# Dividing the attention by its softmax sums behind the mixing, with the sums turned by TensorE and read back from DRAM

## The chip, the cores and the metric

One core of a Trainium2 chip runs the whole program. The metric is the time of one execution on the device, in microseconds; lower is better. A core has five engines with a queue of instructions each: TensorE (PE in the profile; PEld are its weight loads), VectorE (DVE), ScalarE (ACT), GpSimd (POOL) and SyncE (SP), which issues nearly all transfers between DRAM and the on-chip memory. Matmuls write to PSUM, eight banks of 128 partitions by 512 numbers; the other memory, SBUF, holds everything else.

## The reference

Two residual layers over 512 frames of 1024 channels. Layer 0 mixes frames by a causal pooling, layer 1 by attention over chunks of 64 frames; a gated feed-forward network with a causal convolution follows each. The change lies in the attention of layer 1, 16 heads of 64 channels:

```python
s = jnp.einsum('bqhd,bkhd->bhqk', qc, kb).astype(jnp.float32) * scale + bias[None]
valid = (band_chunk + c - LEFT_CHUNKS) >= 0
s = jnp.where(valid[None, None, None, :], s, -1e30)
p = jax.nn.softmax(s, axis=-1).astype(vb.dtype)
return jnp.einsum('bhqk,bkhd->bqhd', p, vb)
```

The softmax divides each row (a frame that asks, q) by the sum of its exponentials over the frames that are looked at (k). Behind the attention the 16 heads' outputs are joined to 1024 channels and multiplied with the matrix `w_o`.

## The kernel before

Products of full precision are made of three matmuls with numbers split into a high and a low part (`hi` and `lo`; helper `split`, L102 on ACT for the high part and L103 on DVE for the low part; `load_split` loads a weight and splits it, the weights wo of pairs 0 to 5 both parts on POOL, L100 and L103). `mm3` at L123 to L125 issues the three.

The attention runs in the loop of L1430 to L1487, over 64 tiles: 16 heads times 4 row tiles of 128 frames. Two heads are a pair p, 0 to 7. Tile t of a head sees the 128 x (t + 1) frames up to its own. In step i of the loop PE is given, in this order:

- `scores(tile i)`: two matmuls sc (L1394, L1395), then DVE adds the bias B and takes the minimum (L1398), ACT takes Exp with the row's sum (L1400), DVE the reciprocal of the sum (L1401), and ACT multiplies the tile by it (L1402). Numbers of the tile lie as sb, with the frames q on the partitions, so that a sum is one number for each partition.
- `channel_major` in two steps of each pair: queries (zh, z) and keys (kl) of the next pair are turned (zt) and scaled; halves of them are moved over the partitions by four DMAs on SP.
- `turn(tile i - 2)`: transposes of the tile's 128x128 blocks (tp, L1410), so that k lies on the partitions, and a split into pt0h, pt0l or pt1h, pt1l (for the even or odd head).
- `mix(head)`, when tile i - 4 is a head's last: the matmuls oo (L1422) of the values with pt; ACT copies half (ob, L1427) and DVE adds (L1428) into `O2[p]`, a tile o of 128 x 512 with the pair's 128 channels on the partitions and the frames q along the row.

Behind each of these a filler puts other matmuls on PE: the products for queries and keys of the later pairs (qk<-wqk) up to step 35, then the output product (wo<-two,wo_h), 144 matmuls, from about step 35.5 on. The output product of pair p reads the split of `O2[p]`, which lies in two (XS[p] and XS[8 + p]); the split is issued at the end of a step, when the pair's last tile has been mixed (L1481 to L1483).

The order on PE is the one in which the code issues the work (`manual_schedule`). On DVE, ACT, POOL and SP a scheduler sets the order at compile time, by its own estimate of what is ready when. Each engine then works its queue strictly in order.

PSUM: the tags P and Q hold the fillers' products, four banks under the tag S serve sc, zt, tp and oo in turn.

Of the kernel before, what the change touches and what calls it, by code (L numbers as in the profile page):

```python
# [17 lines left out]
F32 = mybir.dt.float32  # L18
F32R = mybir.dt.float32r
AF = mybir.ActivationFunctionType  # L20
# [3 lines left out]
P = 128  # L24
S = 512
# [5 lines left out]
HD = 64  # L31
NPAIR = H // 2
TT = S // P
# [39 lines left out]
def trunk(ctx: ExitStack, tc: tile.TileContext, xt, xT, cols, band, edge, poolw, gv, wout, wqk, wv, wo, rel, out):  # L73
    nc = tc.nc
# [3 lines left out]
    tmp = ctx.enter_context(tc.tile_pool(name="tmp", bufs=1))  # L78
    dram = ctx.enter_context(tc.tile_pool(name="dram", bufs=1, space=bass.MemoryType.DRAM))
# [9 lines left out]
    def psum(tag, name, bufs=2):  # L89
        return ps.tile([P, S], F32, name=name, tag=tag, bufs=bufs)  # L90
# [3 lines left out]
    def g_tile(name):  # L94
        return tmp.tile([P, S], F32, name=name, tag="g", bufs=6)
# [31 lines left out]
    def run(steps):  # L127
        step = None
        for step in steps:
            pass  # L130
        return step
# [9 lines left out]
    def small(name, n, tag="nw"):  # L141
        return tmp.tile([P, n], F32, name=name, tag=f"{tag}{n}", bufs=4)
# [211 lines left out]
    ident = consts.tile([P, P], F32, name="ident")  # L354
    col = consts.tile([P, NCOL], F32, name="col")
    ones = consts.tile([P, 1], F32, name="ones")
    gq = consts.tile([P, 2], F32, name="gq")
    rdram = dram.tile([H, RLEN], F32, name="rdram")
    ET = mybir.EngineType
    with tc.tile_pool(name="start", bufs=1) as sp, tc.manual_schedule(engines={ET.PE, ET.DVE, ET.Activation, ET.Pool, ET.SP}):  # L360
        first, second, acc0 = mixer(sp)

    def ffn(l, first, pool, acc, summed=None, upool=None, hook=None):
# [56 lines left out]
        def early():  # L420
# [6 lines left out]
            for at, (f, k, i) in enumerate(units):  # L427
# [13 lines left out]
                if at == (19, 14)[l]:  # L441

                    order = tc.manual_schedule(engines={ET.DVE, ET.Activation}) if l == 0 else nullcontext()
                    order.__enter__()
# [388 lines left out]
        def tour():  # L833
# [8 lines left out]
            def place(f, k):  # L842

                for word in PLACES[k].split():
                    x, name = word.split(".")
                    step = steps_of(f + "qofn".index(x) - 2).get(name)
                    if step:
                        step()

            for f in range(KIND.index("s"), NF + 2):  # L850
# [10 lines left out]
                for k in range(7):  # L861
                    if (f, k) == (ORDERED, 0):
                        order.enter_context(tc.manual_schedule(engines={ET.DVE, ET.Activation, ET.SP}))
                    place(f, k)
# [50 lines left out]
    def attention(rest, hook, hidden_slots):  # L915
        XS = set2
        O2, V, Z, QK, SM = {}, {}, {}, {}, {}
# [440 lines left out]
        def channel_major(p, i):  # L1358


            zt = psum("S", f"zt{p}_{i}", 4)
            for t in range(TT):
                j = 4 * i + 2 * (p % 2)
                nc.tensor.transpose(zt[:, t * P:(t + 1) * P], Z[p // 2, t][:, j:j + 2, :].rearrange("p h d -> p (h d)"), ident)
            zh, z2 = (big.tile([P, S], F32R, name=f"z{c}{p}_{i}", tag="zqk", bufs=8) for c in "h2")
            zl = None if i else g_tile(f"zl{p}_{i}")
            if i:
                nc.scalar.activation(zh, zt, AF.Copy, scale=gq[:, i:i + 1])
                for e in range(2):
                    hs = slice(e * HD, (e + 1) * HD)  # L1370
                    nc.vector.scalar_tensor_tensor(KL[p % 2][e][hs], zt[hs], gq[hs, i:i + 1], zh[hs].bitcast(F32), op0=OP.mult, op1=OP.subtract)
            else:
                split_scaled(zt, gq[:, i:i + 1], zh, zl)

            nc.gpsimd.tensor_copy(z2[HD:], zh[HD:].bitcast(F32))
            moves = [(z2[:HD], (z2 if i else zl)[HD:]), (zh[HD:], (zh if i else zl)[:HD])]
            for o, x in moves:
                nc.sync.dma_start(o.bitcast(F32), x if x.dtype == F32 else x.bitcast(F32))
            QK[p, i] = (zh, z2)

        def scores(h, t):

            p, e = divmod(h, 2)
            q, k, kl = QK[p, 0][e], QK[p, 1][e], KL[p % 2][e]
            if t == 0:

                base = rdram[h, :]
                for r, n in ((0, S - HD), (HD, S)):
                    nc.sync.dma_start(BT[h % 2][r:r + HD, S - n:], bass.AP(tensor=base.tensor, offset=base.offset + HD, ap=[[1, HD], [1, n]]))
            n = (t + 1) * P  # L1390
            nw = max(n, 256)

            sc = psum("S", f"sc{h}_{t}", 4)
            nc.tensor.matmul(sc[:, :nw], q[:, t * P:n], k[:, :nw], start=True, stop=False)  # L1394
            nc.tensor.matmul(sc[:, :nw], q[:, t * P:n], kl[:, :nw], start=False, stop=True)  # L1395
            SM[h, t] = s_ = heads.tile([P, n], F32, name=f"sb{h}_{t}", tag=f"sb{t}")
            mx = tmp.tile([P, 3], F32, name=f"mx{h}_{t}", tag="mx", bufs=4)
            nc.vector.tensor_tensor_reduce(out=s_[:, :n], in0=sc[:, :n], in1=BT[h % 2][:, :n][:, ::-1], scale=1.0,  # L1398
                                           scalar=3e38, op0=OP.add, op1=OP.min, accum_out=mx[:, 0:1])
            nc.scalar.activation(s_[:, :n], s_[:, :n], AF.Exp, scale=-1.0, bias=mx[:, 0:1], accum_out=mx[:, 1:2])  # L1400
            nc.vector.reciprocal(mx[:, 2:3], mx[:, 1:2])  # L1401
            nc.scalar.activation(s_[:, :n], s_[:, :n], AF.Copy, scale=mx[:, 2:3])  # L1402

        def turn(h, t):

# [7 lines left out]
        def mix(h):  # L1413

            p, e = divmod(h, 2)
            hs = slice(e * HD, (e + 1) * HD)
            oo = psum("S", f"oo{h}", 4)
            if p not in O2:
                O2[p] = heads.tile([P, S], F32, name=f"o2_{p}", tag="o2", bufs=4)
            for c in range(2):  # L1420
                for j in range(TT):
                    nc.tensor.matmul(oo[:, j * P:], V[j, h // 4][:, h % 4].rearrange("p a d -> p (a d)"),  # L1422
                                     PT[e][c][:, 4 * j:3 * j + TT].rearrange("p t q -> p (t q)"),
                                     start=j == 0 and c == 0, stop=j == TT - 1 and c == 1)
            ob = g_tile(f"ob{h}")
            other = slice(HD - e * HD, 2 * HD - e * HD)
            nc.scalar.activation(ob[hs], oo[other], AF.Copy)  # L1427
            nc.vector.tensor_add(O2[p][hs], oo[hs], ob[hs])  # L1428

        r2, late = small("r2", TT), []  # L1430
        closing = ExitStack()
        with tc.tile_pool(name="pre", bufs=1, reuse_waits="tile") as pre:
            with tc.manual_schedule(engines={ET.PE, ET.DVE, ET.Activation, ET.SP}):
                rcol, second = opening(pre)
        heads = closing.enter_context(tc.tile_pool(name="bh", bufs=1, reuse_waits="tile"))
# [9 lines left out]
        with tc.manual_schedule(engines={mybir.EngineType.PE}):  # L1445
            cur, done, kept = 0, 0, 0

            def fill(upto):

                nonlocal cur, done  # L1450
                while cur < len(fillers):
                    g, n, a, b = fillers[cur]
                    due = n * (upto - a) / (b - a)
                    while done < min(due, n):
                        next(g)
                        done += 1
                    if upto < b:
                        return
                    run(g)
                    cur, done = cur + 1, 0  # L1460

            fill(0)
            for i in range(nb + LAG + LAGM):
                steps = []
                if i < nb:
                    steps.append(lambda: scores(*tiles_[i]))
                if i % 8 in CM and i // 8 + 1 < NPAIR:
                    steps.append(lambda: channel_major(i // 8 + 1, CM.index(i % 8)))
                j = i - LAG
                if 0 <= j < nb:  # L1470
                    steps.append(lambda: turn(*tiles_[j]))
                j2 = j - LAGM
                if 0 <= j2 < nb and j2 % TT == TT - 1:
                    steps.append(lambda: mix(tiles_[j2][0]))
                for x, step in enumerate(steps):
                    step()
                    if late and x < 2:
                        late.pop(0)()
                    fill(i + (x + 1) / len(steps))

                while 8 * kept + 7 <= j2 and (cur == 3 or cur == 2 and done >= 24 * (kept // 2 + 1)):  # L1481
                    split(O2[kept], XS[kept], XS[KD + kept])
                    kept += 1  # L1483
            fill(nb + FO)
# [40 lines left out]
    with tc.tile_pool(name="ba", bufs=1, reuse_waits="tile") as big:  # L1525
        rest = attention(rest, hook, hidden_slots)
# [55 lines left out]
```

## Time and profile before

| | |
|---|---|
| median of the runs | 967.28 us (967.24 to 968.49) |
| the profiled execution | 969.2 us, of it the span 967.4 us |
| PE busy | 956.3 us, 99% of the span |
| DVE busy | 849.5 us, 88% |
| ACT busy | 594.0 us, 61% |
| POOL busy | 91.2 us, 9% |
| attention's loop | about 447 to 604 us of the span |

How to read the profile: one execution was recorded, and the span is the time between its first and its last instruction. A row of the timeline holds the start in us, the duration in us, the engine, the line of the code, the operation, the tiles written and read, the shape and, in brackets, how long the engine was idle ahead of it and what it waited for. A row of grouped instructions holds the count, then the busy time in us and the mean duration in ns, then the idle time of the engine ahead of them and what ended it. The names of tiles stand without their numbers: o is the `O2` of any pair. A wait for several semaphores is put down to the one that came last.

### The profile page before, as it was taken

What the parts mean: (1) busy time and instruction counts of PE and PEld (TensorE: products, weight loads), DVE (VectorE), ACT (ScalarE), POOL (GpSimd) and SP (SyncE); (2) the same over time, 40 slices, a digit from 0 to 9 for tenths busy, and PEclk for the clock granted to TensorE, in tenths of its full rate; (3) what the DMA queues carried; (4) which work ended last, traced back from release to release, by engine and by line L of the source; (5) the groups of instructions that cost most, each with busy time, mean ns of one, the idle gap of its engine ahead of it and who ended that gap; (6) DMA issues with size and microseconds to landing.
All of it is one profiled execution on the core that took longest, in us unless ns stands there. A gap on an engine that the chain in (4) does not pass through costs nothing.

```text
span 967.4 us, 13737 instructions
## 1 busy us (share of the span) xinstructions
PE 956.3 (99%) x4958; PEld 810.0 (84%) x4958; DVE 849.5 (88%) x1522; ACT 594.0 (61%) x1023; POOL 91.2 (9%) x81
## 2 busy tenths in 40 slices
PE   8999999999999999999999999999999999999998
PEld 7788988888888888888888777888988888888886
DVE  8999999999899859895786887999999999989953
ACT  7665554655555457466898888656565565456531
POOL 2300000000000000043525441000000000000000
PEclk9999999999999999999999999999999999999999
DMA  9222332332323317024433341332333233332323
GB/s 343 73 97 71 115 108 81 120 120 80 114 79 120 102 48 292 21 66 133 132 113 97 88 117 55 100 109 80 94 115 108 84 120 111 102 104 79 114 79 111
DMA packets 38996, 103.87 MB, mean 107 GB/s; under 512 B 4464, under 2 KB 7936, under 8 KB 38928
## 3 DMA queue, kind: packets, MB, share of 16 engines
q1 hardware_dynamic: 38864, 102.95, 33.0%
q8 instruction: 39, 0.64, 0.3%
q14 instruction: 29, 0.24, 0.1%
q0 software_dynamic: 32, 0.04, 0.0%
q10 hardware_dynamic: 32, 0.00, 0.0%
HBM read 96.65 MB, written 2.14 MB: 102 GB/s over the span
## 4 chain that ended last, share of the span: by engine, by line
PE 87%; DVE 8%; ACT 2%; DMA 1%; issue 1%; SPq 0%; POOL 0%; DVEq 0%; ACTq 0%; POOLq 0%
PE st_m L593 10%; PE out L124 8%; PE out L125 8%; PE out L123 8%; PE st_m L595 5%; PE st_t L593 5%; PE gv L124 4%; PE gv L125 4%; PE gv L123 4%; PE qk L123 3%; PE qk L124 3%; PE qk L125 3%; PE st_t L595 3%; PE st_b L593 3%; PE tp L1410 1%; PE st_b L595 1%
## 5 line engine op out<-in xcount | busy, mean ns | idle before, releaser
L124 PE MATMUL out<-one,ow_h 128*128 128x512 f32 x224 | 88.1, 393 | 0.0
L123 PE MATMUL out<-one,ow_h 128*128 128x512 f32 x224 | 88.0, 393 | 0.0
L125 PE MATMUL out<-one,ow_l 128*128 128x512 f32 x224 | 87.9, 393 | 0.0
L829 DVE TENSOR_TENSOR X<-out,X 128x512 f32<-128x512 f32 (+1 forms) x65 | 44.3, 683 | 45.9 <-PE out L125 45.6
L593 PE MATMUL st_m<-two,g_h 128*128 128x512 f32 x240 | 75.1, 394 | 0.1
L593 PE MATMUL st_m<-h,g_h 128*128 128x512 f32 x240 | 74.1, 390 | 0.0
L392 ACT ACTIVATE ow_h<-wo_r 128x768 fp32r<-128x768 f32 (+1 forms) x56 | 44.4, 794 | 43.4 <-PE out L124 39.8
L407 DVE SCALAR_TENSOR_TENSOR c<-a,col,c 128x511 f32<-128x511 f32 (+1 forms) x76 | 56.8, 749 | 0.0
L593 PEld LDWEIGHTS st_m<-h,g_h 128*128 128x128 f32 x240 | 45.1, 188 | 10.3
L595 PEld LDWEIGHTS st_m<-two,g_l 128*128 128x128 f32 x240 | 45.0, 188 | 9.6
L593 PEld LDWEIGHTS st_m<-two,g_h 128*128 128x128 f32 x240 | 44.0, 188 | 10.4 <-ACT w L602 0.8
L393 DVE TENSOR_TENSOR ow_l<-wo_r,ow_h 128x768 fp32r<-128x768 f32 (+1 forms) x56 | 50.4, 899 | 2.3 <-ACT ow_h L392 2.3
L602 ACT ACTIVATE w<-st_m 128x512 f32<-128x512 f32 x30 | 18.0, 598 | 55.2 <-PE st_m L595 55.2
L595 PE MATMUL st_m<-h,g_l 128*128 128x256 f32 x240 | 48.3, 283 | 0.0
L595 PE MATMUL st_m<-two,g_l 128*128 128x256 f32 x240 | 47.6, 280 | 0.0
L124 PEld LDWEIGHTS out<-one,ow_h 128*128 128x128 f32 x224 | 42.4, 189 | 5.7 <-DVE one L418 0.3
L125 PEld LDWEIGHTS out<-one,ow_l 128*128 128x128 f32 x224 | 42.4, 189 | 5.5
L123 PEld LDWEIGHTS out<-one,ow_h 128*128 128x128 f32 x224 | 42.4, 189 | 5.4
L1398 DVE CUSTOM_DVE_ANT_0 sb<-sc,B 128x128 f32<-128x128 f32 (+1 forms) x64 | 31.1, 486 | 17.9 <-PE sc L1395 13.3
L404 ACT ACTIVATE c<-a,col 128x512 f32<-128x512 f32 x38 | 30.7, 813 | 23.8 <-DVE a L751 22.2
L392 ACT ACTIVATE g_h<-gv_r 128x1024 fp32r<-128x1024 f32 x32 | 33.7, 1055 | 13.5 <-DMA gv_r<-gv 12.9
L1400 ACT ACTIVATE sb<-sb,mx 128x128 f32<-128x128 f32 (+1 forms) x64 | 35.7, 558 | 9.8 <-DVE mx L1398 9.2
(459 smaller groups left out, 3035.7 us busy)
## 6 DMA issues: line engine op xcount, KB each, us to landing
gv_r<-gv SPq DMA_DIRECT2D x86, 512.0 KB, 3.9
wo_r<-wout SPq DMA_DIRECT2D x32, 384.0 KB, 3.1
wo_r<-wout SPq DMA_DIRECT2D x32, 320.0 KB, 2.9
wqk_r<-wqk SPq DMA_DIRECT2D x12, 512.0 KB, 3.5
b<-wv SPq DMA_DIRECT2D x8, 512.0 KB, 6.7
wo_r<-wo SPq DMA_DIRECT2D x8, 512.0 KB, 3.6
xt<-xt SPq DMA_DIRECT2D x4, 512.0 KB, 5.2
X<-xT SPq DMA_DIRECT2D x8, 256.0 KB, 7.5
```

The lines of the kernel that those rows point to most:

```text
L123: yield nc.tensor.matmul(o, sh, mh, start=first, stop=False, **how)
L124: yield nc.tensor.matmul(o, sh, ml, start=False, stop=False, **how)
L125: yield nc.tensor.matmul(o, sl, mh, start=False, stop=last, **how)
L392: nc.scalar.activation(hi[:, :n], raw[:, :n], AF.Copy)
L393: return hi, lo, lambda: nc.vector.tensor_sub(lo[:, :n], raw[:, :n], hi[:, :n].bitcast(F32))
L404: nc.scalar.activation(c, a, AF.Identity, scale=cw[2], bias=cw[3])
L407: nc.vector.scalar_tensor_tensor(c[:, j:], a[:, :S - j], cw[2 - j], c[:, j:], op0=OP.mult, op1=OP.add)
L593: nc.tensor.matmul(o, hi[:, c], B[i, name], start=first and i == 0, stop=False, **how)
L595: nc.tensor.matmul(o[:, 0], lo[:, c], B[i, name][:, 0], start=False, stop=i == 3, **how)
L829: nc.vector.tensor_add(X[d][:, fs], o[:, fs], X[d][:, fs])
L1398: nc.vector.tensor_tensor_reduce(out=s_[:, :n], in0=sc[:, :n], in1=BT[h % 2][:, :n][:, ::-1], scale=1.0, scalar=3e38, op0=OP.add, op1=OP.m ...
L1400: nc.scalar.activation(s_[:, :n], s_[:, :n], AF.Exp, scale=-1.0, bias=mx[:, 0:1], accum_out=mx[:, 1:2])
```

## The change

For pairs 0 to 6 (called 1 to 7 by their count) the tiles are no longer multiplied by the reciprocals of their sums. Exp leaves its row sum in a column of `sums[p]`, 128 x 8, one column for each of the pair's eight tiles, and one reciprocal is taken behind the eighth. The tiles are turned and mixed as they are, and the pair's output o is divided afterwards. There the frames lie along the row, not on the partitions, so the eight columns have to be turned and spread:

- `sums_out(p)`, ahead of the scores of step 8p + 9: PE transposes the 128 x 8 reciprocals to 8 x 128 (rt, a bank of tag S), ACT copies them to rs, SP writes rs to DRAM (rinv, 4 KB).
- `sums_in(p)`, step 8p + 11: two reads of SP bring them back as rb, 128 x 512, each row of 512 repeated over the 64 partitions of its head.
- `scale(p)`, step 8p + 15: POOL multiplies o by rb.

The split of o for pairs 0 to 6 is issued four steps later than before, behind the multiplication. `O2` has three buffers, and had four. Pair 7 keeps its scales and reciprocals. In all PE has 7 transposes more, ACT 56 scales less and 7 copies more, DVE 56 reciprocals less and 7 more, POOL 7 multiplications more, SP 7 writes and 14 reads more.

```diff
-            nc.scalar.activation(s_[:, :n], s_[:, :n], AF.Exp, scale=-1.0, bias=mx[:, 0:1], accum_out=mx[:, 1:2])
-            nc.vector.reciprocal(mx[:, 2:3], mx[:, 1:2])
-            nc.scalar.activation(s_[:, :n], s_[:, :n], AF.Copy, scale=mx[:, 2:3])
+            if p < NPAIR - 1:
+                if e == 0 and t == 0:
+                    sums[p] = tmp.tile([P, 2 * TT], F32, name=f"sums{p}", tag="sums", bufs=2)
+                c = e * TT + t
+                nc.scalar.activation(s_[:, :n], s_[:, :n], AF.Exp, scale=-1.0, bias=mx[:, 0:1], accum_out=sums[p][:, c:c + 1])
+                if c == 2 * TT - 1:
+                    nc.vector.reciprocal(sums[p], sums[p])
+            else:
...
+        def sums_out(p):
+
+            rt = psum("S", f"rt{p}", 4)
+            nc.tensor.transpose(rt[:2 * TT, :P], sums.pop(p), ident)
+            rs = heads.tile([2 * TT, P], F32, name=f"rs{p}", tag="rs")
+            nc.scalar.activation(rs, rt[:2 * TT, :P], AF.Copy)
+            nc.sync.dma_start(rinv[p], rs)
+
+        def sums_in(p):
+
+            RB[p] = heads.tile([P, S], F32, name=f"rb{p}", tag="rb")
+            for b in range(2):
+                nc.sync.dma_start(RB[p][b * HD:(b + 1) * HD], rinv[p, b * TT:(b + 1) * TT, :].rearrange("c q -> (c q)")[None].to_broadcast([HD, S]))
+
+        def scale(p):
+            nc.gpsimd.tensor_mul(O2[p], O2[p], RB.pop(p))
...
-                O2[p] = heads.tile([P, S], F32, name=f"o2_{p}", tag="o2", bufs=4)
+                O2[p] = heads.tile([P, S], F32, name=f"o2_{p}", tag="o2", bufs=3)
...
+                p = (i - 9) // 8
+                if 0 <= p < NPAIR - 1 and (i - 9) % 8 in (0, 2, 6):
+                    (sums_out, sums_in, scale)[(i - 9) % 8 // 2 - (i - 9) % 8 // 6](p)
...
-                while 8 * kept + 7 <= j2 and (cur == 3 or cur == 2 and done >= 24 * (kept // 2 + 1)):
+                while 8 * kept + (11 if kept < NPAIR - 1 else 7) <= j2 and (cur == 3 or cur == 2 and done >= 24 * (kept // 2 + 1)):
```

Where the scheduler puts the split of pair 4's output on DVE. Before, it stood between a turned tile of head 10 (pt0l) and the scores of head 11 (sb_2) (o_4 is pair 4's output, two its low part, sc and sb are tiles of the scores):

```order
L1398 ISA sb_1_5769,mx_1_5770<-sc_1_5766,B_4307 128x256
L1398 ISA mx_1_5770 128x1
L103 TENSOR_TENSOR pt0l<-tp_2_5756,pt0h 128x3x128
L103 TENSOR_TENSOR two_102<-o_4_5605,two_98 128x512
L1401 RECIPROCAL mx_1_5770<-mx_1_5770 128x1
L1398 ISA sb_2_5789,mx_2_5790<-sc_2_5786,B_4307 128x384
```

And now, with the reciprocal over the eight sums of pair 5 (sums) ahead of it:

```order
L1349 TENSOR_TENSOR X_75<-wo_0_5727,X_75 128x512
L103 TENSOR_TENSOR pt1l<-tp_1_5773,pt1h 128x2x128
L1407 RECIPROCAL sums_5593<-sums_5593 128x8
L103 TENSOR_TENSOR two_102<-o_4_5570,two_98 128x512
L1399 ISA sb_0_5809,mx_0_5810<-sc_0_5806,B_4307 128x128
L1399 ISA mx_0_5810 128x1
L1454 TENSOR_TENSOR o_5_5780<-oo_5779,ob_5789 64x512
```

The split moved back, from between two tiles of pair 5 to behind the last tile of that pair, ahead of the scores of head 12 (sb_0).

On POOL, around the multiplication of pair 3's output o_3 (wo_0_h and wo_0_l are the two parts of a weight of the output product, z_0 and z_1 halves of queries and keys). Before:

```order
L1375 CAST z_0_5439<-zh_0_5438 64x512
L100 CAST wo_0_h<-wo_0_r 128x1024
L1375 CAST z_1_5475<-zh_1_5474 64x512
L103 TENSOR_TENSOR wo_0_l<-wo_0_r,wo_0_h 128x1024
L1321 TENSOR_TENSOR z_0_5386<-z_0_5386,qk_y 128x512
```

And now:

```order
L1376 CAST z_0_5411<-zh_0_5410 64x512
L100 CAST wo_0_h<-wo_0_r 128x1024
L1376 CAST z_1_5448<-zh_1_5447 64x512
L1428 TENSOR_TENSOR o_3_5322<-o_3_5322,rb_5427 128x512
L103 TENSOR_TENSOR wo_0_l<-wo_0_r,wo_0_h 128x1024
L1322 TENSOR_TENSOR z_0_5357<-z_0_5357,qk_y 128x512
```

The multiplication came in ahead of wo_0_l, which has to wait for it.

On SP, where a weight of the output product (wo_4_r) is loaded beside the moves of pair 6's queries and keys (z, zh). Before:

```order
L1378 DMA z_0_5684<-zl_0_5685 64x512
L1389 DMA B_4306<-rdram 64x448
L1389 DMA B_4306<-rdram 64x512
L1378 DMA zh_0_5683<-zl_0_5685 64x512
L117 DMA wo_4_r<-wo 128x4x256
L1378 DMA z_1_5714<-z_1_5714 64x512
L1378 DMA zh_1_5713<-zh_1_5713 64x512
```

And now:

```order
L1419 DMA rinv<-rs_5608 8x128
L1425 DMA rb_5665<-rinv 64x512 x2
L1390 DMA B_4307<-rdram 64x448
L1390 DMA B_4307<-rdram 64x512
L1379 DMA z_0_5651<-zl_0_5652 64x512
L1379 DMA zh_0_5650<-zl_0_5652 64x512
L1379 DMA z_1_5682<-z_1_5682 64x512
L1379 DMA zh_1_5681<-zh_1_5681 64x512
L117 DMA wo_4_r<-wo 128x4x256
```

The load of wo_4_r went from between the moves to behind the last of them, and the way of pair 4's reciprocals through DRAM came in ahead of them.

More of the change, by code (lines that the diff above doesn't have):

```diff
@@ L358, in trunk @@
     rdram = dram.tile([H, RLEN], F32, name="rdram")
+    rinv = dram.tile([NPAIR, 2 * TT, P], F32, name="rinv")
     ET = mybir.EngineType
@@ L1399, in scores @@
                                            scalar=3e38, op0=OP.add, op1=OP.min, accum_out=mx[:, 0:1])
-            nc.scalar.activation(s_[:, :n], s_[:, :n], AF.Exp, scale=-1.0, bias=mx[:, 0:1], accum_out=mx[:, 1:2])
-            nc.vector.reciprocal(mx[:, 2:3], mx[:, 1:2])
-            nc.scalar.activation(s_[:, :n], s_[:, :n], AF.Copy, scale=mx[:, 2:3])
+            if p < NPAIR - 1:
[6 more added lines that the diff above has]
+            else:
+                nc.scalar.activation(s_[:, :n], s_[:, :n], AF.Exp, scale=-1.0, bias=mx[:, 0:1], accum_out=mx[:, 1:2])
+                nc.vector.reciprocal(mx[:, 2:3], mx[:, 1:2])
+                nc.scalar.activation(s_[:, :n], s_[:, :n], AF.Copy, scale=mx[:, 2:3])
+        def sums_out(p):
[10 more added lines that the diff above has]
+            nc.gpsimd.tensor_mul(O2[p], O2[p], RB.pop(p))
         def turn(h, t):
@@ L1428, in mix @@
             nc.vector.tensor_add(O2[p][hs], oo[hs], ob[hs])
-        r2, late = small("r2", TT), []
+        r2, late, sums, RB = small("r2", TT), [], {}, {}
         closing = ExitStack()
```

## The prediction

> **What bounds the kernel now.** I read the chain of waits first, then the windows of the attention, then the waits of TensorE (PE), then the timeline at each of them.
>
> ```profile
> PE 87%; DVE 8%; ACT 2%; DMA 1%; issue 1%; SPq 0%; POOL 0%; DVEq 0%; ACTq 0%; POOLq 0%
> ```
>
> PE carries the chain, so an operation taken from ACT or DVE is worth only what PE waited for it. Two windows of the attention's loop show where that is (the columns: us, then busy us and number of PE, PEld, DVE, ACT, POOL, then the granted clock).
>
> ```profile
> 447.00:538.00 91.00, 91.00 (x497) 76.64 (x497) 62.76 (x190) 78.11 (x187) 39.21 (x29) 1.00 0.37 109
> 538.00:604.00 66.00, 61.82 (x347) 50.37 (x346) 55.85 (x159) 55.46 (x141) 24.21 (x19) 1.00 0.31 87
> L1402 ACT ACTIVATE sb<-sb,mx 128x128 f32<-128x128 f32 (+1 forms) x64 | 35.5, 556 | 3.8 <-DVE mx L1401 3.0
> PE tp L1410 <- ACT sb L1402: 3.2, 5, 1.7
> ```
>
> Up to 538 us PE is busy for 91.00 of 91.00 us: what the change takes from ACT there is worth nothing. From 538 to 604 it is idle for 4.18 us. The change removes 56 of the 64 scales (31 us of ACT) and 56 of the 64 reciprocals, but PE waited for a scale only 5 times, for 3.2 us in all (the longest 1.7). These places count, and the sum is made from starts of matmuls.
>
> **The pace of PE.** The price of an added transpose, and of a 512-column matmul without a wait:
>
> ```profile
> 525.59 0.40 PE L125 MATMUL qk<-wqk_h,two 128*128 128x512 f32 x1
> 525.83 0.27 PE L1410 MATMUL tp<-ident,sb 128*128 128x128 f32 x1
> 525.85 0.48 PE L123 MATMUL qk<-wqk_h,two 128*128 128x512 f32 x1
> 526.17 0.39 PE L124 MATMUL qk<-wqk_l,two 128*128 128x512 f32 x1
> 526.40 0.40 PE L125 MATMUL qk<-wqk_h,two 128*128 128x512 f32 x1
> ```
>
> A step from one matmul to the next takes 0.23 to 0.24 (526.17 to 526.40). From 525.59 to 526.40 lie three such steps and one transpose: 0.81 - 3 x 0.23 = 0.12 for the transpose, though its row says 0.27.
>
> **What is removed.** The places in order; behind each pair of rows the distance of the starts less 0.23.
>
> ```profile
> 543.85 0.40 PE L125 MATMUL wo<-two,wo_l 128*128 128x512 f32 x1
> 544.50 0.33 PE L1410 MATMUL tp<-ident,sb 128*128 128x128 f32 x1 [0.25 <-ACT sb L1402]
> ...
> 545.84 0.40 PE L123 MATMUL wo<-two,wo_h 128*128 128x512 f32 x1
> 546.51 0.49 ACT L1402 ACTIVATE sb<-sb,mx 128x256 f32<-128x256 f32 x1
> 547.05 0.44 PE L1410 MATMUL tp<-ident,sb 128*128 128x128 f32 x2 [0.82 <-ACT sb L1402]
> ...
> 564.48 0.40 PE L124 MATMUL wo<-two,wo_h 128*128 128x512 f32 x1
> 565.17 0.35 PE L1394 MATMUL sc<-zh,zh 128*128 128x256 f32 x1 [0.30 <-DMA zh<-zh]
> ...
> 571.84 0.47 PE L124 MATMUL wo<-two,wo_h 128*128 128x512 f32 x1
> 572.34 0.76 PE L1422 MATMUL oo<-pt1h,one 128*128 128x512 f32 x3
> ...
> 578.84 0.40 PE L123 MATMUL wo<-two,wo_h 128*128 128x512 f32 x1
> 580.89 0.43 PE L1410 MATMUL tp<-ident,sb 128*128 128x128 f32 x2 [1.65 <-ACT sb L1402]
> ...
> 586.77 0.40 PE L123 MATMUL wo<-two,wo_h 128*128 128x512 f32 x1
> 587.33 0.33 PE L1410 MATMUL tp<-ident,sb 128*128 128x128 f32 x1 [0.17 <-ACT sb L1402]
> ```
>
> At 544.50 0.42 and at 547.05 0.98: the scale of the tile ended late (the second ran from 546.51, on an ACT that had other work until then), and without a scale the transposes wait for Exp alone, which had ended by then. At 565.17 0.46, a wait for the move of zh. At 572.34 0.27, where DVE and ACT are late with the split in front of the mixing; of it I take 0.2, as both lose work there but keep the split. At 580.89 1.82. At 587.33 0.33: pair 7 keeps its scales, but ACT in front of them has fewer. Sum: 4.2 us.
>
> The wait at 565.17 has its cause on SP:
>
> ```profile
> 557.40 0.54 SPq L117 DMA_DIRECT2D wo_r<-wo  x1
> ...
> 558.70 0.54 SPq L1378 DMA_DIRECT2D zh<-zh  x1
> ```
>
> The move was issued at 558.70, behind a load of 512 KB. In the changed order that load stands behind both moves of that pair, so I take the 0.46 as gone. If the 14 rows new on SP held the move up as long, 0 to 0.46 would stay.
>
> The wait at 580.89 has its cause on DVE and POOL:
>
> ```profile
> 577.28 2.38 POOL L103 TENSOR_TENSOR wo_l<-wo_r,wo_h 128x1024 fp32r<-128x1024 f32 x1
> 577.29 2.92 DVE L103 TENSOR_TENSOR two<-o,two 128x512 fp32r<-128x512 f32 x1
> ...
> L103 DVE TENSOR_TENSOR two<-o,two x8: 682/683/2918, 505.4 to 605.8; 128x512 fp32r<-128x512 f32 x8
> ```
>
> The subtraction two<-o of the split takes 0.683 in the median, and 2.92 here, beside POOL's wo_l: it ends 0.55 behind POOL. What stood behind it on DVE, a reciprocal first, was 2.24 late; PE lost 1.82. So DVE's lateness reaches PE less about 0.42. **This is the term on which the sum turns**, since the change moves two<-o and POOL's operations against each other, and does not part them.
>
> The Trainium skill, "SBUF — State Buffer", section "SBUF: two separate sides", has a rule that speaks against this change: GpSimd and a DVE operation with two inputs from SBUF share a pair of ports, the first holds it for its whole instruction and the other blocks. The rows above agree, 2.92 against 0.683; by that rule each of the seven new multiplications on POOL is one more holder, which is the second rival.
>
> **What is added.** Seven transposes rt on PE, each just ahead of a scores matmul: 7 x 0.12 = 0.84. The sums are complete ahead of each (for pair 5 at about 564.4, below, with rt ahead of 566.74), so they wait for nothing new. Bounds: 0, where PE waits there anyway, and 7 x 0.27 = 1.9 by the row's length.
>
> The Trainium skill, "TensorE: Matmul & The Clock Gate", section "Part 4: PE-mode transpose", gives some 275 ns for one within a kernel; the row's 0.27 agrees, and with it the sum would end 1.1 higher, but the starts show 0.12.
>
> Then the three places where wo_l and DVE meet anew.
>
> ```profile
> 539.97 2.39 POOL L103 TENSOR_TENSOR wo_l<-wo_r,wo_h 128x1024 fp32r<-128x1024 f32 x1
> 541.59 0.70 DVE L1428 TENSOR_TENSOR o<-oo,ob 64x512 f32<-64x512 f32 x1
> 543.92 0.17 DVE L1316 TENSOR_TENSOR qk_a<-qk_s,r 128x32 f32<-128x32 f32 x1
> ...
> L1321 POOL TENSOR_TENSOR z<-z,qk_y 128x512 f32<-128x512 f32 x12 | 12.6, 1082 | 14.6 <-DVE qk_y L1319 14.6
> ```
>
> (a) Pair 3: POOL's multiplication of o_3 stands ahead of wo_l now and waits for the addition that ends at 542.29. It takes 1.08 (like the z rows), so wo_l runs from 543.4 to 545.8 in place of 539.97 to 542.36. DVE's qk_a, two inputs from SBUF, comes at 543.92 and is held 1.8; less 0.42, PE waits 1.4.
>
> ```profile
> 563.39 0.72 ACT L1400 ACTIVATE sb<-sb,mx 128x512 f32<-128x512 f32 x1
> 563.93 2.38 POOL L103 TENSOR_TENSOR wo_l<-wo_r,wo_h 128x1024 fp32r<-128x1024 f32 x1
> 565.69 0.29 DVE L1398 CUSTOM_DVE_ANT_0 sb<-sc,B 128x128 f32<-128x128 f32 x1 [1.26 <-PE sc L1395]
> 566.74 0.28 PE L1394 MATMUL sc<-zh,zh 128*128 128x256 f32 x1
> ```
>
> (b) Pair 4: two<-o_4 moves behind the reciprocal over the sums of pair 5, which waits for the Exp that ends at 564.1. So it starts at about 564.4, inside wo_l (to 566.31), and ends 0.55 behind it, at 566.9. The sb of head 12 behind it began at 565.69: 1.2 late, less 0.42 is 0.8 for PE.
>
> ```profile
> 574.96 0.69 DVE L1428 TENSOR_TENSOR o<-oo,ob 64x512 f32<-64x512 f32 x1
> 576.15 1.04 POOL L100 CAST wo_h<-wo_r 128x1024 fp32r<-128x1024 f32 x1 [2.96 <-issue]
> ```
>
> (c) Pair 5: the multiplication of o_5 waits for the addition that ends at 575.65, and wo_h and wo_l stand behind it: wo_l from 577.8 to 580.2. Two<-o_5, now further back on DVE (at about 578.6), ends at 580.75 in place of 579.3: 1.45, less 0.42 is 1.0. Each of (a) to (c) lies between 0 (DVE arrives outside wo_l) and the 2.24 that the full collision held DVE. I take the values above, from the order and these starts.
>
> The way through DRAM is the new wait for POOL. Nothing in the trace has its shape; the nearest rows:
>
> ```profile
> outT<-X SPq DMA_DIRECT2D x7, 256.0 KB, 2.0
> B<-rdram SPq DMA_DIRECT2D x16, 128.0 KB, 3.1
> ```
>
> For pair 5 rt runs just ahead of the scores that began at 566.74; 0.27 for it, 0.6 for ACT's copy (the scales' mean is 556 ns), 2.0 for the write, twice 0.54 to issue the reads and 3.1 for them: rb lands at about 573.8, ahead of 575.65, for which POOL waits in any case. So it costs 0, with 1.9 of cover; without it the excess comes once at each of pairs 4 to 6, up to 2 each if the two transfers took twice as long. SP waits for the write with the reads of B behind it, which have a head's time to come. The seven multiplications run on a POOL that is free for most of the loop, and nobody on PE waits for them before the product of that pair.
>
> **Sum:** -4.2 + 0.84 + 1.4 + 0.8 + 1.0 = -0.2 us. The profiled execution took 969.2 us (span 967.4 and 1.8 around it), so by itself it becomes 969.0; the median of the runs is 967.28, 1.9 lower, and becomes **967.1**.
>
> **The rivals.**
> *The waits go and nothing comes for them.* Then -4.2 + 0.84: 963.9. For it: ACT loses 31 us of work, and with it DVE could pass wo_l earlier or later than I place it. Against: wo_l takes 2.4 us at each place. Chance 0.2.
> *POOL holds DVE in full* at (a), (b) and (c): 2.24 each without the 0.42, 6.7 + 0.84 - 4.2 = +3.3: 970.6. It makes the kernel slower by over 0.2% (about what a measurement of this kernel can tell from no change) from 1.8 us a place. For it: the 2.92 row, and that PE's banks are all waited for there. Against: POOL's multiplications take 1.08 only. Chance 0.15.
> *The change doesn't do what it says:* the scales were not what PE waited for, but DVE behind them; the same gaps stay under another name, and the transposes are on top: 967.28 + 0.84 = 968.1. For it: the longest wait came from two<-o. Against: at 544.50 and 547.05 DVE was done. Chance 0.15.
>
> **How the numbers follow.** The forecast, an exchange of old waits for new ones, has 0.5, within 965.4 to 968.6 by itself. Faster by over 0.2% (under 965.35) is the first rival and 0.06 of the forecast: 0.26; slower by over 0.2% (above 969.2) the second and 0.03: 0.18; the rest 0.56. The range takes in the first rival and the third, and stops short of the second in full: 963.6 to 969.8.
>
> **What would show it.** After the change the five waits for L1402 must be gone up to 581 (right in any case but the third rival). (a): qk_a of about 2 us near 544 and PE idle behind it. (b): the two<-o near 564.4 of over 2 us. (c): one near 579. Without these three long rows the first rival holds. The starts around each rt must show 0.12; 0.27 would be 1 us more. If POOL's multiplications wait for rb and not for DVE's addition, the cover of the round trip was wrong. I would be wrong altogether if PE showed waits before 538, where it had none.

## The result, and the profile after

| | before | with the change |
|---|---|---|
| median of the runs | 967.26 us (966.46 to 968.49) | 972.9 us (972.27 to 973.41) |
| ratio, 95% interval | | 1.0056 (1.0040 to 1.0072) |
| the profiled execution | 969.2 us, span 967.4 | 973.41 us, span 971.6 |

The change makes the kernel slower by 5.6 us, 0.6%. The forecast was no change (967.1 us) in a range up to 969.8.

The chain of the changed kernel, its windows that answer to those shown of before, one more near the end of the program, and the scales and reciprocals that are left (L1411 and L1410 are the old L1402 and L1401):

```profile
PE 90%; DVE 7%; issue 1%; ACT 1%; DMA 1%; SPq 0%; DVEq 0%; ACTq 0%
...
447.00:538.00 91.00, 91.00 (x498) 76.54 (x497) 57.95 (x156) 62.96 (x153) 43.46 (x31) 1.00 0.38 114
538.00:604.00 66.00, 63.21 (x353) 50.99 (x353) 57.98 (x144) 47.27 (x125) 30.34 (x24) 1.00 0.37 109
930.00:960.00 30.00, 30.00 (x131) 24.16 (x130) 12.79 (x18) 6.67 (x9) 0.00 (x0) 1.00 0.36 112
...
L1411 ACT ACTIVATE sb<-sb,mx 128x128 f32<-128x128 f32 (+3 forms) x8 | 4.4, 551 | 0.1
L1410 DVE RECIPROCAL mx<-mx 128x1 f32<-128x1 f32 x8 | 1.3, 157 | 0.9 <-ACT sb L1409 0.8
```

The scales take 4.4 us of ACT in place of 35.5, and PE's idle time from 538 to 604 us fell from 4.18 to 2.79 us. So in this pair of profiles the attention did get shorter: the same matmul (the first ones behind the attention, at 625 us) starts 1.0 us later than in the profile of before, but the matmuls ahead of the attention (at 444 us) started 1.2 us later already. What was lost was lost elsewhere. The last matmul starts 4.1 us later, and 3.1 of them come behind the attention, in a feed-forward layer that the change does not touch. About 0.5 us of these is one wait, which the profile of before doesn't have:

```profile
905.40 0.73 PE L594 MATMUL st_m<-two,g_h 128*128 128x512 f32 x2 [0.53 <-ACT v L603]
```

The row 930:960 shows the rest: PE is busy all the time, at a granted clock of 1.00, and the row counts 131 matmuls in 30 us. The same window before:

```profile
930.00:960.00 30.00, 30.00 (x134) 24.86 (x133) 12.37 (x17) 6.77 (x9) 0.00 (x0) 1.00 0.34 108
```

It counts 134. (A row counts a matmul that overlaps an end of its window too; from start to start, the steps in it are 227 ns in the mean before and 232 now.) Nothing waits; each matmul steps a little more slowly.

The three places that the prediction named in the attention are there. First (a), pair 3:

```profile
543.68 1.28 POOL L1428 TENSOR_TENSOR o<-o,rb 128x512 f32<-128x512 f32 x1 [2.26 <-DVE o L1454]
544.92 2.40 POOL L103 TENSOR_TENSOR wo_l<-wo_r,wo_h 128x1024 fp32r<-128x1024 f32 x1
...
545.11 2.25 DVE L1317 TENSOR_TENSOR qk_a<-qk_s,r 128x32 f32<-128x32 f32 x1
...
546.80 0.39 PE L123 MATMUL wo<-two,wo_h 128*128 128x512 f32 x1
548.32 0.41 PE L1436 MATMUL tp<-ident,sb 128*128 128x128 f32 x2 [1.13 <-ACT pt1h L102]
```

POOL's multiplication waits for DVE's addition (not for rb), wo_l comes behind it, DVE's qk_a takes 2.25 us beside it in place of 0.17, and PE waits: 548.32 - 546.80 - 0.23 = 1.29 us. Then (b), pair 4:

```profile
565.85 2.39 POOL L103 TENSOR_TENSOR wo_l<-wo_r,wo_h 128x1024 fp32r<-128x1024 f32 x1
...
566.12 0.21 DVE L1407 RECIPROCAL sums<-sums 128x8 f32<-128x8 f32 x1
566.64 2.15 DVE L103 TENSOR_TENSOR two<-o,two 128x512 fp32r<-128x512 f32 x1 [0.32 <-ACT two L102]
568.72 0.28 DVE L1399 CUSTOM_DVE_ANT_0 sb<-sc,B 128x128 f32<-128x128 f32 x1
...
568.18 0.27 PE L1416 MATMUL rt<-ident,sums 128*8 128x128 f32 x1
569.06 0.38 PE L1395 MATMUL sc<-zh,zh 128*128 128x256 f32 x1 [0.61 <-DVE mx L1399]
```

Two<-o behind the reciprocal of the sums takes 2.15 us beside wo_l in place of 0.68, sb comes late behind it, and the scores matmul starts 0.88 behind rt. At the rt of pairs 0 to 4, where nothing waits, that step takes 0.03, so the wait is 0.85. And (c), pair 5:

```profile
580.29 2.40 POOL L103 TENSOR_TENSOR wo_l<-wo_r,wo_h 128x1024 fp32r<-128x1024 f32 x1
...
580.85 2.40 DVE L103 TENSOR_TENSOR two<-o,two 128x512 fp32r<-128x512 f32 x1
...
584.87 0.40 PE L123 MATMUL wo<-two,wo_h 128*128 128x512 f32 x1
585.35 0.27 PE L1416 MATMUL rt<-ident,sums 128*8 128x128 f32 x1
```

The same collision; PE loses 0.25 us ahead of rt (585.35 - 584.87 - 0.23) and 0.13 behind it.

### The profile page after: what moved, and what is told of

It reads as the page before. It is cut to its first block, busy times and chain, and to the rows that moved or that the text cites. A ratio compares the mean times of both kernels' runs of the same rounds, so it can differ in the third digit from the quotient of the medians.

```text
span 971.6 us, 13722 instructions
## 1 busy us (share of the span) xinstructions
PE 962.3 (99%) x4965; PEld 810.0 (83%) x4965; DVE 847.7 (87%) x1473; ACT 570.2 (59%) x974; POOL 100.7 (10%) x88
## 4 chain that ended last, share of the span: by engine, by line
PE 90%; DVE 7%; issue 1%; ACT 1%; DMA 1%; SPq 0%; DVEq 0%; ACTq 0%
PE st_m L594 10%; PE out L124 8%; PE out L125 8%; PE out L123 8%; PE st_m L596 5%; PE st_t L594 5%; PE gv L124 4%; PE gv L123 4%; PE gv L125 4%; PE qk L125 3%; PE qk L123 3%; PE qk L124 3%; PE st_t L596 3%; PE st_b L594 3%; PE tp L1436 2%; PE oo L1448 2%
## 5 line engine op out<-in xcount | busy, mean ns | idle before, releaser
L1405 ACT ACTIVATE sb<-sb,mx 128x128 f32<-128x128 f32 (+3 forms) x56 | 31.3, 559 | 21.6 <-DVE mx L1399 21.1
L393 ACT ACTIVATE g_h<-sa 128x1024 fp32r<-128x1024 f32 x32 | 33.8, 1057 | 11.8 <-DVE sa L639 7.3
```

Of the source, the lines that this page charges most:

```text
L393: nc.scalar.activation(hi[:, :n], raw[:, :n], AF.Copy)
```

## The experiments

Two questions: why PE's matmuls outside the attention step more slowly, and what the attention itself gained or lost. For the first there was one suspect. The new tiles for the sums, 8 numbers of 4 bytes in two buffers, take 64 bytes a partition in the pool of temporaries, which is allocated once for the whole program: the tiles of the pools that are opened behind it in SBUF moved by 64 bytes, those of the feed-forward layers too.

**A dummy of 64 bytes, and the change without the shift.**

```diff
 kernel before, in scores():
+            if (h, t) == (0, 0):
+                tmp.tile([P, 16], F32, name="pad", tag="pad", bufs=1)
```

> The kernel before with a tile of 64 bytes a partition more in the pool of temporaries, that nothing reads or writes: every tile behind it in SBUF lies 64 bytes further, as in the change, and no instruction differs. Theory layout (the 64 bytes of the tiles for the sums shift the operands of the feed-forward products off multiples of 128 bytes, and their matmuls step at 230 to 234 ns in place of 227): 970.5 to 973 us. Theory work (the added transposes, transfers and POOL's multiplications cost the time): 967.3 us as before.

Measured: 970.81 us against 967.12 for the kernel before in the same job, ratio 1.0038 (1.0023 to 1.0053).

```diff
 the change:
-                    sums[p] = tmp.tile([P, 2 * TT], F32, name=f"sums{p}", tag="sums", bufs=2)
+                    sums[p] = heads.tile([P, 2 * TT], F32, name=f"sums{p}", tag="sums", bufs=2)
```

> The change as it is, but the tiles for the sums are taken from the pool of the attention, so that nothing outside the attention is shifted. Theory layout: 966.5 to 967.5 us, with an offset against the kernel before that stays below 0.5 us up to the attention and after it. Theory work: 972.9 us as the change.

Measured: 969.14 us, ratio 1.0023 (1.0013 to 1.0033): between the two theories. An unused tile costs 3.7 us, and the change without the shift still costs 2.0. Together 5.7, the whole loss (5.6). So both theories hold, each for its share. With its sums in the attention's pool the change is also free of the wait at 905.40.

**Which shift.** The dummy with 32 and 64 numbers in place of 16 (128 and 256 bytes), and the change with wider tiles for the sums (128 and, with 8 * TT columns, 256 bytes in both buffers together; the reciprocal and the transpose read the first eight columns alone):

```diff
-                    sums[p] = tmp.tile([P, 2 * TT], F32, name=f"sums{p}", tag="sums", bufs=2)
+                    sums[p] = tmp.tile([P, 4 * TT], F32, name=f"sums{p}", tag="sums", bufs=2)
```

> The kernel before with a tile of 128 bytes more at the same place. Theory layout, if it is the place within 128 bytes that matters: 967.3 us. If any shift matters (which tiles lie in which part of the memory): over 969 us. Theory work: 967.3 us.

> The change with tiles for the sums of twice the width (the upper half not used), so that everything behind them is shifted by 128 bytes in place of 64. Theory layout, place within 128 bytes: 966.5 to 967.5 us. If any shift matters: over 969 us. Theory work: 972.9 us.

> The kernel before with a tile of 256 bytes a partition more at the place of the 64 and 128 bytes. If the operands' place within 256 bytes matters: 967.2 us. If a multiple of 512 bytes or more is needed, or any shift costs: 969 to 970 us.

> The change with tiles for the sums of four times the width (the rest of each not used), so that everything behind them lies 256 bytes further. Theory layout (an operand's place within 256 bytes) with 2.0 us from the attention itself: 968.7 to 969.3 us. Rival (the attention's share also came from the layout of its own tiles): 967.2 us. Rival (the layout needs more than multiples of 256 bytes): 971 us or more.

| shift of what lies behind | kernel before with a dummy | the change |
|---|---|---|
| 0 | 967.1 | 969.14 (a_heads) |
| 64 bytes | 970.81 | 972.9 |
| 128 bytes | 969.65, ratio 1.0029 (1.0018 to 1.0040) | 971.65, ratio 1.0049 (1.0032 to 1.0066) |
| 256 bytes | 966.87, ratio 0.9998 (0.9989 to 1.0007) | 968.8, ratio 1.0019 (1.0010 to 1.0028) |

A shift of 128 bytes still costs 2.5 us, so the theory of a place within 128 bytes was wrong; one of 256 costs nothing that can be told. The change costs 1.9 to 2.1 us more than the dummy in each row. The window near the end, of the kernel before with 64 bytes, with 256, and of the change with its sums in the attention's pool:

```profile
930.00:960.00 30.00, 30.00 (x130) 24.13 (x129) 12.34 (x17) 6.78 (x9) 0.00 (x0) 1.00 0.33 107
```

```profile
930.00:960.00 30.00, 30.00 (x134) 24.82 (x133) 11.91 (x17) 5.58 (x8) 0.00 (x0) 1.00 0.35 117
```

```profile
930.00:960.00 30.00, 30.00 (x134) 24.84 (x133) 12.35 (x17) 6.63 (x9) 0.00 (x0) 1.00 0.33 108
```

130, 134 and 134 matmuls: the pace goes with the place in memory and not with the change. To see whose place it is, the steps from a 512-column matmul to the next matmul outside the attention (steps over 260 ns left out) are sorted by where its moving operand and the next one's weights begin within 256 bytes. The places are those of the built programs; the traces hold no addresses. The table has the matmuls whose operands both begin at 0 in the kernel before, by where they begin with the dummy of 64 bytes, and the mean of the same steps in both executions:

| moving operand at, weights at | steps | mean before | mean with the dummy |
|---|---|---|---|
| 0, 0 | 910 | 228.5 ns | 229.4 ns |
| 0, 64 | 807 | 230.1 ns | 233.5 ns |
| 64, 0 | 397 | 227.5 ns | 230.5 ns |
| 64, 64 | 322 | 229.5 ns | 231.9 ns |

So a step gets longer by 2.4 to 3.4 ns where an operand moved off, and by 0.9 where neither did. With the dummy of 256 bytes the same 2436 steps have the mean that they had before, 229.0 ns.

**The matmuls that lay off before.** The kernel before has 189 steps with a moving operand (u) at 224 within 256 bytes, mean 232.8 ns, and 150 with weights (g) at 128, mean 232.9; the other 2436 are those of the table, at 229.0. If their own place is the reason, moving them must pay:

```diff
 kernel before:
-    tmp.tile([P, 32], F32, name="fill1")
+    tmp.tile([P, 64], F32, name="fill1")
...
+        if upool:
+            upool.tile([P, 56], F32, name="fillu")
...
+            if (h, t) == (0, 0):
+                tmp.tile([P, 32], F32, name="pad", tag="pad", bufs=1)
```

> The kernel before with three tiles that nothing uses (128 bytes at two places, 224 on the right side), so that the operands of the feed-forward products that lay off multiples of 256 bytes (u as the moving operand, 192 matmuls at 232.8 ns, and 120 of the weights g at 128, at 233 ns) come to lie on them, with no other instruction. Theory layout: they step at 229 ns like the others, about 300 x 3.8 ns = 1.2 us less: 966.0 us. Rival (these matmuls are slower for another reason): 967.2 us.

Measured: 965.94 us, ratio 0.9989 (0.9980 to 0.9998), 1.2 us less than before. In its trace all but a handful of these steps are of the kind (0, 0), 2766 with a mean of 229.1 ns.

**What a usual execution of before looks like.** The attention's own 2.0 us did not fit: in the two profiles it was shorter.

> The kernel before, profiled once more. Theory race (in the execution whose profile the prediction read, POOL's wo_l began 10 ns ahead of DVE's two<-o at 577.28 and PE lost 1.82 us behind it; in a usual execution DVE begins first and loses nothing): an execution of 966.5 to 967.7 us, two<-o at that place of about 0.68 us, wo_l of about 2.95 us, and no wait of PE over 0.3 us near 580. Rival (the wait belongs to every execution): two<-o of 2.9 us and the wait of 1.8 us again.

Measured: 967.27 us. The place of the longest wait, in this execution of the same kernel:

```profile
577.34 0.68 DVE L103 TENSOR_TENSOR two<-o,two 128x512 fp32r<-128x512 f32 x1
...
577.36 2.92 POOL L103 TENSOR_TENSOR wo_l<-wo_r,wo_h 128x1024 fp32r<-128x1024 f32 x1
...
538.00:604.00 66.00, 63.78 (x360) 52.67 (x359) 55.88 (x165) 56.70 (x143) 24.82 (x19) 1.00 0.32 90
...
PE tp L1410 <- ACT sb L1402: 1.5, 4, 0.8
```

Here DVE began 0.02 us ahead of POOL, two<-o took its 0.68, wo_l took 2.92 in place of 2.4, and PE did not wait. In the profile that the prediction read POOL was 0.01 us ahead, two<-o took 2.92, and PE lost 1.82 us. PE's idle time in the window is 2.22 us here and was 4.18 there. The dummies of 64, 128 and 256 bytes and b_align show the same as this execution (wo_l of 2.93 to 2.95 us). So the 1.82 us belong to the one profiled execution and not to the usual one. They make up most of what it lay above the median, but the two numbers are not the same thing: the wait for zh (0.46) is not here either, and ahead of the attention this execution had lost 0.6 us more. How often POOL comes first is not known: six of 33 other runs of before took over 968.3 us, and no trace of them was kept.

The Trainium skill, "SBUF — State Buffer", section "SBUF: two separate sides", says that of GpSimd and a DVE operation with two SBUF inputs the one that starts first holds the ports and the other blocks. These two executions agree, 0.02 us one way and 0.01 us the other: each time the later one is longer. Closer than that the records don't tell: with the dummy of 64 bytes both begin at 578.01, POOL's 4 ns ahead, and it is POOL's wo_l that takes 2.95.

Between the traces of b_again and a_heads, two kernels with the same places outside the attention, PE's starts move apart by 2.3 us over the attention. So the 2.0 us that the change loses without the shift are lost in the attention.

**The low part of the split on POOL.**

```diff
 the change with its sums in the attention's pool:
-                    split(O2[kept], XS[kept], XS[KD + kept])
+                    split(O2[kept], XS[kept], XS[KD + kept], nc.gpsimd if kept < NPAIR - 1 else None)
```

> The change with the tiles for the sums in the attention's pool, and the low part of the split of pairs 0 to 6 (two<-o) made by POOL behind its multiplication, in place of DVE. Theory collision (DVE's two<-o is held by POOL's wo_l at pairs 4 and 5, 0.85 and 0.25 us for PE): 967.8 to 968.3 us, without a wait of PE at the scores of head 12. Rival (the round trip through DRAM and the transposes cost it): 969.1 us as with that layout. If the low part comes too late from POOL: over 969.5 us, with PE waiting in wo<-two.

Measured: 968.62 us, ratio 1.0015 (1.0005 to 1.0024), 0.5 less than with DVE. The wait at the scores of head 12 is gone, but at pair 3 POOL is late with the low part:

```profile
L103 POOL TENSOR_TENSOR two<-o,two x7: 1296/1304/1307, 505.3 to 595.9; 128x512 fp32r<-128x512 f32 x7
...
549.39 0.40 PE L123 MATMUL wo<-two,wo_h 128*128 128x512 f32 x1
550.18 0.50 PE L124 MATMUL wo<-two,wo_h 128*128 128x512 f32 x1 [0.39 <-POOL two L103]
```

POOL takes 1.30 us for it (DVE 0.68), from 548.82 on, when ACT has made the high part, and 0.56 us come back there (550.18 - 549.39 - 0.23). So the kernel takes more than the 968.3 us that were expected at most.

**Without the transposes and the way through DRAM.** The reciprocals are not turned or read back; POOL multiplies by a tile of ones, so this kernel leaves out the division of pairs 0 to 6.

```diff
 the change with its sums in the attention's pool:
-            nc.tensor.transpose(rt[:2 * TT, :P], sums.pop(p), ident)
...
+            sums.pop(p)
...
-            RB[p] = heads.tile([P, S], F32, name=f"rb{p}", tag="rb")
...
+            RB[p] = fixed
```

> The change with the tiles for the sums in the attention's pool, without the seven transposes, ACT's copies and the way through DRAM: POOL multiplies by a tile of ones, so that the attention's outputs of pairs 0 to 6 are not divided. Theory collision: the places of (a) and (b) stay, 7 x 0.12 us and the 0.37 us around the rt of pair 5 go: 968.0 us. Rival (the round trip costs it all): 967.1 us or less.

Measured: 967.95 us, ratio 1.0008 (0.9998 to 1.0017), 1.2 less than with them. The wait of (a) stays (1.29 us). The rest is not all the transposes' own time: the wait of (b) falls from 0.85 to 0.27 here, at the transposes behind those scores, and one at pair 7 grows from 0.42 to 0.93. Why these two changed was not tried.

**Pair 3's multiplication on DVE.**

```diff
 the change with a shift of 256 bytes (a_sums256):
-            nc.gpsimd.tensor_mul(O2[p], O2[p], RB.pop(p))
+            (nc.vector if p == 3 else nc.gpsimd).tensor_mul(O2[p], O2[p], RB.pop(p))
```

> The kernel a_sums256 with the multiplication of pair 3's output on DVE in place of POOL, so that POOL's wo_l stands where it stood before the change. Theory collision (a) (DVE's qk_a is held by wo_l, which the multiplication pushed back, and PE waits 1.28 us at its transposes near 547): that wait falls to under 0.4 us and the kernel takes 0.7 to 1.2 us less than a_sums256, near 968.0. Rival (PE waits there for something else): no change.

Measured: 967.17 us, ratio 1.0003 (0.9994 to 1.0012), 1.6 less than a_sums256. The collision is gone:

```profile
541.28 2.40 POOL L103 TENSOR_TENSOR wo_l<-wo_r,wo_h 128x1024 fp32r<-128x1024 f32 x1
...
543.96 0.68 DVE L1428 TENSOR_TENSOR o<-o,rb 128x512 f32<-128x512 f32 x1
545.49 0.18 DVE L1317 TENSOR_TENSOR qk_a<-qk_s,r 128x32 f32<-128x32 f32 x1
...
553.86 0.33 PE L1365 MATMUL zt<-ident,z 128*128 128x128 f32 x1 [0.67 <-POOL z L1322]
```

Wo_l is over before qk_a comes, qk_a takes 0.18, and PE's 1.29 us are gone. The gain is larger than expected because DVE's order behind it changed too: two<-o of pair 4 now comes behind the scores of head 12, takes 0.99, and the 0.85 of (b) is gone as well; a new wait for POOL's z at 553.86 gives 0.7 back.

**All of it.** All multiplications on DVE, the low part for pairs 4 to 6 on POOL, and the alignment of b_align:

```diff
-            nc.gpsimd.tensor_mul(O2[p], O2[p], RB.pop(p))
+            nc.vector.tensor_mul(O2[p], O2[p], RB.pop(p))
...
-                    split(O2[kept], XS[kept], XS[KD + kept])
+                    split(O2[kept], XS[kept], XS[KD + kept], nc.gpsimd if 4 <= kept < NPAIR - 1 else None)
```

> The change with all seven multiplications on DVE, the low part of the split of pairs 4 to 6 on POOL, and all operands of the feed-forward products on multiples of 256 bytes. If (a), (b) and (c) go (1.28 + 0.85 + 0.37 us) and the layout gains 1.3: 965.5 to 966.3 us. If DVE, with 0.68 us more for each pair, is late in front of the split and the scores: 967 us or more.

Measured: 966.12 us, ratio 0.9987 (0.9978 to 0.9996). PE no longer waits at (a) to (c), but the wait for POOL's z of 0.67 us is here too. The time beats both kernels', and is no better than b_align (965.94 us): the idea of the change, freed of its collisions, is worth nothing that these runs can tell beside the alignment alone.

## Why the prediction was wrong

The forecast was 967.1 us and the time 972.9, 5.8 more. Two steps failed.

**The larger one is a term that was missing: 3.7 us for 64 bytes in a pool.** The prediction costed every instruction added or removed, and put at nothing, without a reason, what the new tiles do to the addresses of all that lies behind them. None of its rivals had it. An unused tile of 64 bytes alone costs 3.7 us, and without that shift the change takes 969.14 us, inside the range.

**The other is the last step, from the sum to the median: 2.0 us.** The working took 1.82 us at 580.89 as removed, from a profiled execution of 969.2 us, and then went over to the median by taking off the 1.9 us by which that execution lay above it. But that execution lay so high mainly by this wait: POOL 0.01 us ahead of DVE. It was taken off twice. Against the usual execution the sum is -0.2 + 1.8 = +1.6, and the change without the shift measured +2.0.

Against the profiled execution the sum came out right: the attention got 0.3 us shorter between the two profiles (offset 1.24 us ahead of it, 0.98 behind it), forecast 0.2. Part of that is luck. The price of (c) was 0.6 too high, the 0.2 at 572.34 was not gained, and new waits of 0.2 and 0.3 that the sum didn't have came in (at the matmuls of 555.84 and 589.02 in the old timeline).

The other steps:

- *Nothing to be gained up to 538 us:* right, 91.00 of 91.00 again.
- *The waits at 544.50 and 547.05 go:* right, the first is gone, and the second gave way to (a).
- *The wait for zh at 565.17 goes, 0.46:* it is not in the changed profile; but the execution b_again of the kernel before hasn't got it either, and the dummy of 128 bytes has (0.57). So this term, too, may be no part of a usual execution; how often it comes was not tried.
- *572.34, 0.2 less:* wrong, 0.26 is still there at the same step of the program.
- *587.33, 0.33 less:* gone as forecast (the same transpose starts 0.23 behind the matmul ahead of it, at 588.14), but the next tile's transposes, at 590.04, now wait 0.39 for their scale, where they lost 0.13 before.
- *(a) 1.4, (b) 0.8, (c) 1.0:* measured 1.29, 0.85, and 0.25 ahead of rt with 0.13 behind it. The mechanism was right at all three; only (c) was too large.
- *The collision's price, DVE's delay less 0.42:* right at (a) (2.25 - 0.17 = 2.1, and 1.29 for PE) within 0.4, too high at (c).
- *The transposes, 0.12 each:* 0.10 each up to 538 us, from the offset between before and a_heads over four of them (0.04 us ahead of them, 0.44 behind them).
- *The round trip costs nothing:* right; POOL's multiplications wait for DVE's addition, never for rb, whose reads land in 2.7 us (estimated 3.1). The multiplication takes 1.29 us where 1.08 was taken.
- *The rivals:* the waits did not go for nothing (963.9), POOL did not hold DVE in full (970.6), and the change did what it says. The time lies above the second rival, but not by its mechanism.

What stays open: why an operand off a multiple of 256 bytes makes the step longer by 2 to 4 ns, and why the steps of matmuls that did not move get 0.9 longer beside them. The runs show that the pace goes with the place, and that moving those operands alone gives the expected 1.2 us; they don't show what reads or writes more slowly.

## What to carry to other kernels

Where the profiled execution lies above the median, find what it holds that a usual one does not before a term is taken off it, with a second profile if there is one; a race of two engines decided by 10 to 20 ns is such a thing. When a change adds a tile, look at where every other tile goes: a small tile in a pool that lives for the whole program moves all that is allocated behind it, and with its size rounded up to 256 bytes that cost nothing here. On a kernel whose one engine is busy throughout, taking 31 us from another is worth only the few waits, and moves the collisions rather than removing them.

## What the runs showed of the hardware

- Matmuls of 512 columns step at 229.1 ns in the mean with moving operand and weights on multiples of 256 bytes, and at 230.5 to 233.5 ns off them; three shifts of the same program gave +3.7 us (64 bytes), +2.5 (128) and none (256).
- DVE's two<-o and POOL's wo_l, both on two SBUF tiles, hold each other up both ways: two<-o 2.92 us and wo_l 2.4, or two<-o 0.68 and wo_l 2.92, as the one or the other starts 10 to 20 ns earlier. Even a 128x32 operation of 0.17 us took 2.25 us beside wo_l.
